# A hybrid layer in float32 on one core: its order computed anew, moving operands shifted to start on 16 bytes, inverses grown four heads at a time, and sums over tiles issued in one go

## The chip, the core and the metric

The kernel runs on one core of a Trainium2 chip. The core has five engines, each with its own queue of instructions that it works through strictly in order: PE (TensorE, the products), DVE (VectorE), ACT (ScalarE), POOL (GpSimd) and SP (which issues the transfers). An instruction that waits for a semaphore holds up everything behind it on its engine. The metric is the device time of one execution in microseconds (us); lower is better.

## What is computed

One layer of a hybrid encoder on 512 tokens behind 16 learned meta tokens, width 1024, all in float32. Cut to what matters here:

```python
u = rmsnorm(h); proj = u @ w_in                      # 1024 x 10256
y_conf = silu(layernorm(causal_dwconv31(c_val * sigmoid(c_gate)))) @ w_conf_out
q, k, v = silu(causal_dwconv4(q, k, v)); q, k = l2norm(q), l2norm(k)
o = chunk_gated_delta_rule(q, k, v, g, beta)         # 8 heads; each chunk needs (I + a_kk)^-1
y_dn = (rmsnorm(o) * silu(z)) @ w_dn_out
h = h + (sigmoid(g_conf) * y_conf + sigmoid(g_dn) * y_dn) @ w_out
u2 = rmsnorm(h); up = causal_dwconv3(u2 @ w_up)      # 1024 x 5632
h = h + (silu(f_gate) * f_val) @ w_down              # 2816 x 1024
return rmsnorm(h)[:, 16:]
```

## The kernel before

**Large products.** Features lie on the 128 partitions and tokens along the free dimension. Every weight block is loaded as a raw tile `wr`, cast by ACT to `wh` and reduced by DVE to the rest `wl`; activations are split in the same way (`uh`/`ul`, `oh`/`ol`, `hh`/`hl`, and so on). A product is the sum of three: (wh, high), (wh, low), (wl, high). The helper `gemm` (L483) issues them: for each of 8 k-tiles and 3 pairs, one PE product for each of two token ranges, so 48 products to an output tile of 128 features, in two PSUM banks (pool `p2`, two such tiles). The two ranges are what the change shifts. `FULL`, `RAW` and `HALO` (264 or 268 columns; tiles k, q, v, cg, cv) already start on multiples of 4 elements, which is 16 bytes. `LATE` and `MIDR` (L539, 258 columns; tiles z and ga, y and wo) start the first range on such a multiple and the second 8 bytes behind one. `UPR` (L1144, 258 columns; the 44 tiles `up` of the feed-forward layer) starts both 8 bytes behind one. The `dn` tiles take 512 aligned columns, the last of them 2 x 256.

**Inverses.** For each of the 8 heads there are four chunks of 128 tokens, and for each chunk a triangular matrix of 128 x 128 has to be inverted. DVE does the 32 x 32 blocks of all heads together (`inverses`, L812); they come back through memory as the tile `DU`. `grow` (L856), called once for each head, makes 64 and then 128 out of 32: DVE transposes blocks into `LL`, ACT copies blocks into `Mn[h]` (tile `mn`), PE makes the 32 x 32 products `gP`, ACT moves them out as `gp`, PE makes the 32 x 32 products `gX`, ACT moves these into `LL` and `mn`, then the same with 64 x 64 (`gP`, moved as `p`, then `gX`). All of them use a part of the PE array (32 x 32 or 64 x 64); the large products use all of it (128 x 128). A head is 8 + 12 products of 32 x 32 and 4 + 4 of 64 x 64.

**Sums.** Sums over the 128 partitions are PE products with 32 columns of ones (tile `rs`, array 128 x 32). The norm of the first four heads takes 32 of them, that of the last four 16, the two sums of the conformer's layer norm 32 each (`sums`, L501).

**What sets the order.** The program is first recorded, call by call. `Plan.order` (L273) then runs a list scheduler: an engine that comes free takes the ready call of the lowest number, where numbers are the place in the recording plus a table of offsets (`BIAS`), and ready is worked out from prices (`Plan.price`) and latencies. `STAY` is added to a large product's number while PE is in a run of small ones. The result is fixed at build time: each engine's queue. `plan.after` makes a call depend on more than its operands. PSUM tiles of one bank (`p1`) have four slots, `wh` and `wl` two each.

The profile names one line, L427, for all instructions, so that they are told apart by tile and shape. The line that issues them and the loop that calls `grow` are these:

```python
                getattr(engines[o.eng], o.fn)(*(get(x) for x in o.a), **{n: get(x) for n, x in o.k.items()})
...
    for h in range(GROW):
        call(grow, "w", h)
    for h in range(H):
        heads(h)
        if h + GROW < H:
            call(grow, "w", h + GROW)
```

Of the kernel before, what the change touches and what calls it, by code (L numbers as in the profile page):

```python
# [11 lines left out]
F32 = mybir.dt.float32  # L12
# [54 lines left out]
class Vw:  # L67
    """a view of a tile: the steps to it, and the same steps taken on a stand-in to know its bounds"""
# [52 lines left out]
class Op:  # L121
    _fields = ("eng", "fn", "a", "k", "prio", "deps", "succ", "late", "wait", "cost", "ready", "end", "tiles", "lat", "table")
# [11 lines left out]
TABLES = {'Exp': ('exp',), 'Tanh': ('exp', 'silu'), 'Silu': ('silu',), 'Sqrt': ('sqrt',)}  # L134
LAT = {'PE': {'PE': 3, 'DVE': 200, 'ACT': 200, 'POOL': 200, 'SP': 200},
# [15 lines left out]
BIAS = {'k3': -850, 'iv': -1500, 'd0': 150, 'v4': -30, 'v2': 0, 'd7': 1500, 'z1': -320, 't11': -280, 'z5': 0, 't7': 250, 'k0': -250, 'ln': 250, 's7': 30, 'z0': -700, 'o2': -250, 'o5': 100, 'd5': -1850, 'g3': 150, 'd6': -250, 'd1': 2130, 'k2': -30, 'q7': -1720, 'k5': -30, 's4': -730, 'd4': 850, 'w3': -1600, 't2': -600, 'c5': -130, 't8': 60, 'v3': 250, 'o4': -600, 'q6': -250, 'g4': -350, 't4': -100, 'o1': 250, 'q4': -630, 't9': -150, 'z2': -600, 'o0': -600, 'g0': 30, 'q3': 250, 'q5': 700, 'c1': 30, 'c6': -130, 's1': 0, 't15': 200, 't1': -700, 's3': 100, 'y0': 250, 't12': -150, 'o6': 100, 'o3': 250, 'k4': -100, 'w2': 250, 't5': -250, 'v0': 30}  # L151
LNP = 74
IVP = 1265
UP = 519
WP = 144
# [39 lines left out]
class Plan:  # L195
# [18 lines left out]
    def add(self, eng, fn, a, k):  # L214
# [30 lines left out]
        if eng == "ACT" and fn == "activation":  # L245
            o.table = TABLES.get(str(k["func"]).split(".")[-1])
# [1044 lines left out]
```

## Time and profile before

| | us |
|---|---|
| timed runs (3), median | 1048.68 |
| timed runs, lowest and highest | 1046.71, 1049.07 |
| profiled execution, first to last instruction (span) | 1049.7 |
| PE busy in it | 1035.5 |
| DVE busy | 718.3 |
| ACT busy | 474.7 |

The profiled execution has no time of its own beside its span; the span is 1.0 us above the timed median, so a difference worked out on the span is taken over to the median as it is. Busy time is the union of instructions that overlap: a product's record is some 0.28 us long while the next one starts 0.12 us behind it, so what a product costs is read from the distance of starts, not from its duration. A float32 product leaves two records, one in the split form (fp32r) leaves one. The granted clock (PEclk) is 1.00 at 2.4 GHz and 0.50 at 1.2 GHz.

The stages: first norm and keys (0 to 70 us), conformer input and inverses of 32 x 32 (70 to 222), heads with the growth of their inverses (222 to 485), layer norm and outputs (485 to 660), feed-forward layer up (660 to 915) and down (915 to 1037), a tail with the last norm.

### The profile page before, as it was taken

The page shows a single profiled execution, that of the slowest core. Times are in us where ns is not written, and L with a number is a line of the kernel's source. Part 1 is how long each engine was busy: PE and PEld are TensorE (multiplying, and loading weights), DVE is VectorE, ACT ScalarE, POOL GpSimd, SP SyncE. Part 2 cuts the span into 40 slices and gives each one's busy share as a digit, 9 for nine tenths or more (in the row PEclk, how much of TensorE's full clock was granted, in tenths as well). Part 3 has the DMA queues.
Part 4 walks back from the last instruction along what each step waited for, and adds up shares of the span by engine and source line. Part 5 has one row for each costly group of instructions (what it writes and reads, how often), then busy time and mean ns, then how long its engine had stood idle before and what let it go on. Part 6 is the DMA issues. An engine that isn't in the chain of part 4 may idle for free.

```text
span 1049.7 us, 20033 instructions
## 1 busy us (share of the span) xinstructions
PE 1035.5 (99%) x8430; PEld 985.7 (94%) x8430; DVE 718.3 (68%) x1237; ACT 474.7 (45%) x863; POOL 9.5 (1%) x45
## 2 busy tenths in 40 slices
PE   9999999999999999999999999999999999999996
PEld 7999999988989999999999999999999999988885
DVE  6987899984867998985546555666666767623324
ACT  6777622557534466444345234534444443413222
POOL 0011000000000000000000000000000000000000
PEclk9999999987999999999999999999999999999998
DMA  6244323231211232212313343232323232333232
GB/s 223 76 123 110 114 82 111 81 102 42 71 42 61 81 106 98 78 65 76 127 61 122 101 143 99 81 102 81 100 81 101 81 101 81 96 91 91 81 105 81
DMA packets 44042, 98.40 MB, mean 94 GB/s; under 512 B 12720, under 2 KB 19248, under 8 KB 43952
## 3 DMA queue, kind: packets, MB, share of 16 engines
q1 hardware_dynamic: 43952, 97.12, 29.2%
q8 instruction: 66, 1.08, 0.4%
q14 instruction: 24, 0.20, 0.1%
HBM read 93.89 MB, written 3.21 MB: 93 GB/s over the span
## 4 chain that ended last, share of the span: by engine, by line
PE 96%; DVE 1%; ACT 1%; DMA 0%; SPq 0%; issue 0%; POOL 0%; DVEq 0%; POOLq 0%; ACTq 0%
PE up L427 24%; PE dn L427 12%; PE ga L427 9%; PE y L427 9%; PE k L427 5%; PE v L427 5%; PE z L427 5%; PE q L427 4%; PE wo L427 4%; PE cv L427 4%; PE cg L427 4%; PE rs L427 2%; PE o L427 2%; PE gX L427 1%; PE S L427 1%; PE gP L427 1%
## 5 line engine op out<-in xcount | busy, mean ns | idle before, releaser
L427 DVE TENSOR_TENSOR wl<-wr,wh 128x1024 fp32r<-128x1024 f32 x157 | 189.3, 1207 | 160.1 <-PE dn L427 47.8
L427 ACT CAST wh<-wr 128x1024 fp32r<-128x1024 f32 x157 | 162.0, 1037 | 287.5 <-PE up L427 87.8
L427 DVE SCALAR_TENSOR_TENSOR ca<-c,par,ca 128x516 f32<-128x516 f32 (+10 forms) x240 | 177.3, 744 | 7.3 <-ACT ca L427 4.8
L427 PE MATMUL up<-hl,wh 128*128 128x258 f32 x704 | 142.1, 283 | 0.0
L427 PE MATMUL up<-hh,wh 128*128 128x258 f32 x704 | 142.1, 283 | 0.0
L427 PEld LDWEIGHTS up<-hh,wh 128*128 128x128 f32 x704 | 109.0, 190 | 0.2 <-issue 0.2
L427 PEld LDWEIGHTS up<-hl,wh 128*128 128x128 f32 x704 | 108.9, 189 | 0.0
L427 PE MATMUL up<-hh,wl 128*128 128x258 f32 x704 | 92.4, 283 | 0.0
L427 PEld LDWEIGHTS up<-hh,wl 128*128 128x128 f32 x704 | 88.3, 189 | 0.0
L427 DVE TENSOR_TENSOR up<-up,r 128x258 f32<-128x258 f32 x88 | 33.4, 420 | 49.0 <-PE up L427 46.0
L427 DVE SCALAR_TENSOR_TENSOR uy<-up,par,uy 128x512 f32<-128x512 f32 x88 | 65.9, 748 | 1.5
L427 PE MATMUL dn<-fh,wh 128*128 128x512 f32 (+1 forms) x198 | 65.0, 369 | 0.0
L427 PE MATMUL dn<-fl,wh 128*128 128x512 f32 (+1 forms) x198 | 64.9, 369 | 0.0
L427 ACT ACTIVATE uy<-up,par 128x512 f32<-128x512 f32 x44 | 36.0, 817 | 53.8 <-DVE up L427 53.8
L427 PE MATMUL ga<-uh,wh 128*128 128x258 f32 x256 | 58.5, 290 | 0.0
L427 PE MATMUL ga<-ul,wh 128*128 128x258 f32 x256 | 57.9, 289 | 0.0
L427 DVE SCALAR_TENSOR_TENSOR cv<-ra,par,cv 128x528 f32<-128x528 f32 x69 | 51.6, 760 | 0.6 <-ACT cv L427 0.5
L427 PE MATMUL dn<-fh,wl 128*128 128x512 f32 (+1 forms) x198 | 49.8, 370 | 0.0
L427 PE MATMUL ga<-uh,wl 128*128 128x258 f32 x256 | 48.4, 299 | 0.0
L427 PEld LDWEIGHTS dn<-fh,wh 128*128 128x128 f32 x198 | 36.9, 188 | 7.8 <-ACT wh L427 1.2
L427 PEld LDWEIGHTS dn<-fl,wh 128*128 128x128 f32 x198 | 36.9, 188 | 6.9
L427 PEld LDWEIGHTS ga<-ul,wh 128*128 128x128 f32 x256 | 42.2, 189 | 0.8 <-issue 0.6
(284 smaller groups left out, 2238.9 us busy)
## 6 DMA issues: line engine op xcount, KB each, us to landing
wr<-in_win SPq DMA_DIRECT2D x64, 512.0 KB, 3.3
wr<-in_wup SPq DMA_DIRECT2D x44, 512.0 KB, 3.7
wr<-in_wd SPq DMA_DIRECT2D x17, 512.0 KB, 3.6
wr<-in_wdn SPq DMA_DIRECT2D x8, 512.0 KB, 3.2
wr<-in_wco SPq DMA_DIRECT2D x8, 512.0 KB, 3.4
wr<-in_wo SPq DMA_DIRECT2D x8, 512.0 KB, 3.3
wr<-in_wd SPq DMA_DIRECT2D x8, 384.0 KB, 3.1
x<-in_xT SPq DMA_DIRECT2D x8, 264.0 KB, 5.8
```

Of the source, the lines that this page charges most:

```text
L427: getattr(engines[o.eng], o.fn)(*(get(x) for x in o.a), **{n: get(x) for n, x in o.k.items()})
```

## The change

Four things, all in the recording; no product is added or removed, and the counts of PE products by array part are the same (6930 split ones, 790 in float32).

1. `UPR` moves by two elements (the tiles `hh`/`hl` are written two columns later), so that both ranges start on 16 bytes. In `LATE` and `MIDR` the second range starts two columns earlier and is 260 long, the first is written two columns into its bank, and what reads the banks takes columns 2 to 260 of both.
2. `grow` does four heads in a call (two calls instead of eight). Each group of products waits until everything that the group reads has been written (`written`). ACT moves a whole group out at once.
3. The sums of the heads' norms and of the layer norm wait until all their tiles are there.
4. The scheduler's prices, `STAY` (3000 to 750), the offsets of stages and the clock's thresholds are new, and with them the order on every engine. Of the table of offsets nothing is shown; its rows tell a reader nothing.

```diff
-LOW = 0.4
+RATE = 0.4453
+TURN = {(False, True): 92, (True, False): 105, (True, True): 190}
+LOW = 0.5
...
-STAY = 3000
+STAY = 750
...
-IVP = 1265
+IVP = 1295
...
-WP = 144
+WP = 30
...
-GROW = 3
+NG = 4
...
-            for b, (c0, c1) in enumerate(ranges):
-                PE.matmul(acc[:, b, :c1 - c0], lhsT=w[:, k * P:(k + 1) * P], rhs=a[k0 + k][:, c0:c1],
+            for b, (c0, c1, *at) in enumerate(ranges):
+                p0 = at[0] if at else 0
+                PE.matmul(acc[:, b, p0:p0 + c1 - c0], lhsT=w[:, k * P:(k + 1) * P], rhs=a[k0 + k][:, c0:c1],
                           start=first and i == 0, stop=last and i == len(runs) - 1)
...
-    def sums(ss, width):
+    def sums(ss, width, whole=False):
+        if whole:
+            plan.after = {j for t in ss for _, j, w in t.tl.hist if w}
...
-    LATE = ((PAD + T0, PAD + T0 + HW), (PAD + T0 + HW, PAD + T))
-    MIDR = ((0, HW), (HW, TW))
+    LATE = ((PAD + T0, PAD + T0 + HW, 2), (PAD + T0 + HW - 2, PAD + T, 0))
+    MIDR = ((0, HW, 2), (HW - 2, TW, 0))
+    MID = slice(2, 2 + HW)
...
-    def grow(h):
...
+    def grow(h0):
+        hs, DU = range(h0, h0 + NG), ivt['DU']
+        LL = []
+        for h in hs[::2]:
             l = bt(n="LL")[:, :8 * 64].rearrange("p (q c) -> p q c", q=8)
             G.memset(l[0:32, :, 32:64], 0.0)
             for r, c in ((0, 0), (32, 32), (64, 0)):
                 V.transpose(out=l[r:r + 32, :, c:c + 32], in_=DU[r:r + 32, NC * h:NC * h + 8])
+            LL.append(l)
+        D8 = lambda h: DU[:, NC * h:NC * h + NC]
+        for h in hs:
+            for b in range(4):
+                r = slice(32 * b, 32 * b + 32)
+                S.copy(out=Mn[h][r, :, r], in_=D8(h)[r])
+        def written(*ts):
+            plan.after = {j for t in ts for _, j, w in t.tl.hist if w}
+        each = [(h, q, (h - h0) * NC + q) for h in hs for q in range(NC)]
         a = p1("gP")
+        written(*LL, *(Mn[h] for h in hs))
+        for h, q, i in each:
+            c, l = slice(i * 32, (i + 1) * 32), LL[i // 8][:, i % 8]
+            PE.matmul(a[32:64, c], lhsT=Mn[h][0:32, q, 32:64], rhs=l[0:32, 0:32], start=True, stop=True)
+            PE.matmul(a[96:128, c], lhsT=Mn[h][64:96, q, 96:128], rhs=l[64:96, 0:32], start=True, stop=True, tile_position=(64, 96))
+        pp = bt(n="gp")
+        n = NG * NC * 32
+        for r in (slice(32, 64), slice(96, 128)):
+            S.copy(out=pp[r, :n], in_=a[r, :n])
         x = p1("gX")
+        written(pp)
+        for h, q, i in each:
+            c, d = slice(i * 32, (i + 1) * 32), D8(h)
+            PE.matmul(x[0:32, c], lhsT=pp[32:64, c], rhs=d[32:64, q], start=True, stop=True)
+            PE.matmul(x[64:96, c], lhsT=pp[96:128, c], rhs=d[96:128, q], start=True, stop=True, tile_position=(96, 64))
+            PE.matmul(x[32:64, c], lhsT=d[32:64, q], rhs=pp[32:64, c], start=True, stop=True)
+        x8 = x[:, :n].rearrange("p (q i) -> p q i", i=32)
+        for i, l in enumerate(LL):
+            S.copy(out=l[32:64, :, 0:32], in_=x8[32:64, 8 * i:8 * i + 8])
+        for h in hs:
+            for r, c in ((slice(0, 32), slice(32, 64)), (slice(64, 96), slice(96, 128))):
+                S.copy(out=Mn[h][r, :, c], in_=x8[r, (h - h0) * NC:(h - h0 + 1) * NC])
+        p64s = []
+        for g in range(NG // 2):
+            a = p1("gP2")
+            written(*LL, *(Mn[h] for h in hs))
+            for h, q, i in each[8 * g:8 * g + 8]:
+                PE.matmul(a[64:128, i % 8 * 64:i % 8 * 64 + 64], lhsT=Mn[h][0:64, q, 64:128], rhs=LL[g][0:64, i % 8], start=True, stop=True)
+            p64 = bt(n="p64")
+            S.copy(out=p64[64:128, :512], in_=a[64:128])
+            p64s.append(p64)
+        for g in range(NG // 2):
+            x = p1("gX2")
+            written(*p64s)
+            for h, q, i in each[8 * g:8 * g + 8]:
+                c = slice(i % 8 * 64, i % 8 * 64 + 64)
+                PE.matmul(x[0:64, c], lhsT=p64s[g][64:128, c], rhs=Mn[h][64:128, q, 64:128], start=True, stop=True)
+            for h in hs[2 * g:2 * g + 2]:
+                S.copy(out=Mn[h][0:64, :, 64:128], in_=x[0:64, (h % 2) * 256:(h % 2 + 1) * 256].rearrange("p (q i) -> p q i", q=NC))
...
+                plan.after = {j for pair in st_r for t in pair for _, j, w in t.tl.hist if w}
...
-    for h in range(GROW):
-        call(grow, "w", h)
+    call(grow, "w", 0)
     for h in range(H):
         heads(h)
-        if h + GROW < H:
-            call(grow, "w", h + GROW)
+        if h == 0:
+            call(grow, "w", NG)
...
-        acc, r = sums(cacc[::-1], TW)
+        acc, r = sums(cacc[::-1], TW, True)
...
-        rl = rstd_sb(sq, TW, 1.0 / D, eps, "rl")
+        rl = rstd_sb(sq, TW, 1.0 / D, eps, "rl", True)
...
+    HS = 2
...
-        S.mul(out=hi[:, :TW], in_=x[:, :TW], mul=pc('nf', f))
-        V.scalar_tensor_tensor(out=lo[:, :TW], in0=x[:, :TW], scalar=pc('nf', f), in1=hi.bitcast(F32)[:, :TW],
+        S.mul(out=hi[:, HS:HS + TW], in_=x[:, :TW], mul=pc('nf', f))
+        V.scalar_tensor_tensor(out=lo[:, HS:HS + TW], in0=x[:, :TW], scalar=pc('nf', f), in1=hi.bitcast(F32)[:, HS:HS + TW],
                                op0=ALU.mult, op1=ALU.subtract)
         hh.append(hi)
...
-    UPR = ((2, 260), (258, 516))
+    UPR = ((HS + 2, HS + 260), (HS + 258, HS + 516))
```

What this does to the queues is seen in three places. `DU`, `gp`, `mn`, `LL` are the tiles named above; `hsel` are the columns of ones for the heads' sums, `o` and `q` the squares that are summed.

**PE, the sums of the first four heads.** Before:

```order
L427 MATMUL S_3_3811<-w_6_3801,kdm_930 128x128
L427 MATMUL o_3_3813<-Em_1000,w_6_3801 128x16
L427 MATMUL gX_3817<-DU_2902,gp_3805 32x32
L427 MATMUL rs_3819<-o_1_3454,hsel_71 32x129
L427 MATMUL gX_3817<-DU_2902,gp_3805 32x32
L427 MATMUL rs_3819<-o_1_3454,hsel_71 32x129
L427 MATMUL gX_3817<-gp_3805,DU_2902 32x32
```

Now:

```order
L447 MATMUL v_4520<-uh_101,wh_4339 128x264
L447 MATMUL rs_4548<-o_1_3506,hsel_71 32x129 x4
L447 MATMUL rs_4548<-q_1_2428,hsel_71 32x129 x4
L447 MATMUL rs_4548<-o_2_3740,hsel_71 32x129 x4
L447 MATMUL rs_4548<-q_2_3440,hsel_71 32x129 x4
L447 MATMUL rs_4548<-o_3_4228,hsel_71 32x129 x4
L447 MATMUL rs_4548<-q_3_3585,hsel_71 32x129 x4
L447 MATMUL rs_4548<-o_4_4535,hsel_71 32x129 x4
L447 MATMUL rs_4548<-q_4_4389,hsel_71 32x129 x4
L447 MATMUL w_9_4586<-v_5_4551,Tm_2216 16x128
```

Before, 24 of these 32 sums stand one by one between products of the growth (16 in this place, 8 in a second one); now all 32 stand together, and the 16 of the last four heads too.

**PE, the growth of the first heads, from the 32 x 32 products to the 64 x 64 ones.** Before:

```order
L427 MATMUL gX_3059<-DU_2902,gp_3043 32x32 x2
L427 MATMUL gX_3059<-gp_3043,DU_2902 32x32
L427 MATMUL ga_2915<-ul_121,wh_2850 128x258
L427 MATMUL ga_2915<-uh_125,wh_2850 128x258 x2
L427 MATMUL ga_2915<-ul_127,wh_2850 128x258 x2
L427 MATMUL ga_2915<-uh_87,wl_2874 128x258
L427 MATMUL gP_1_3096<-LL_2943,mn_1096 64x64 x4
L427 MATMUL gP_2_3102<-LL_2950,mn_1351 64x64 x4
L427 MATMUL ga_2915<-uh_87,wl_2874 128x258
```

Now:

```order
L447 MATMUL gX_3126<-DU_2909,gp_3116 32x32 x2
L447 MATMUL gX_3126<-gp_3116,DU_2909 32x32
L447 MATMUL gP_1_3203<-LL_2994,mn_1059 64x64 x4
L447 MATMUL gP_1_3203<-LL_2994,mn_1138 64x64 x4
L447 MATMUL gP_2_3216<-LL_3000,mn_1200 64x64 x4
L447 MATMUL gP_2_3216<-LL_3000,mn_1234 64x64 x4
L447 MATMUL z_3229<-uh_87,wh_2981 128x258
L447 MATMUL z_3229<-uh_87,wh_2981 128x260
L447 MATMUL z_3229<-ul_90,wh_2981 128x258
L447 MATMUL z_3229<-ul_90,wh_2981 128x260
L447 MATMUL z_3229<-uh_93,wh_2981 128x258
L447 MATMUL gX_1_3241<-mn_1059,p_1_3227 64x64 x4
```

Before, products of `ga` stand between the last `gX` of 32 x 32 and the first `gP` of 64 x 64; now nothing stands there.

**ACT, beside the same place.** Before:

```order
L427 COPY mn_1430<-DU_2902 32x4x32
L427 COPY LL_2943<-gX_3028 32x4x32
L427 COPY mn_1096<-gX_3028 32x4x32 x2
L427 COPY LL_2943<-gX_3049 32x4x32
L427 COPY mn_1247<-gX_3049 32x4x32
L427 COPY LL_2950<-gX_3059 32x4x32
L427 COPY mn_1351<-gX_3059 32x4x32 x2
L427 COPY mn_1247<-gX_3049 32x4x32
L427 COPY mn_1430<-DU_2902 32x4x32 x2
L427 COPY p_1_3112<-gP_2_3102 64x256
```

Now:

```order
L447 COPY gp_3116<-gP_3073 32x512 x2
L447 COPY mn_1616<-DU_2909 32x4x32 x3
L447 COPY mn_1702<-DU_2909 32x4x32 x4
L447 COPY mn_1750<-DU_2909 32x4x32 x4
L447 COPY LL_2994<-gX_3126 32x8x32
L447 COPY LL_3000<-gX_3126 32x8x32
L447 COPY mn_1059<-gX_3126 32x4x32 x2
L447 COPY mn_1138<-gX_3126 32x4x32 x2
L447 COPY mn_1200<-gX_3126 32x4x32 x2
L447 COPY mn_1234<-gX_3126 32x4x32 x2
L447 CAST wh_3201<-wr_2903 128x1024
L447 ACTIVATE gt_3225<-ga_2919,par_69 128x516
```

Before, the copies out of `gX` follow each other with one block copy from `DU` among them; now eleven block copies for the second four heads stand between `gp` and the ten copies that the 64 x 64 products read.

At the end of the queues the norm of the first half of the tokens is moved forward as well: its four products `rb` stand 38 products before the last `dn` one (before: behind it), and so the eight DVE products `fin` of that half stand ahead of the last addition to `xr` instead of behind it.

## Rows read from the trace of the kernel before

**Rows 1.** The page: PE's busy time, its granted clock in slices, the chain.

```profile
PE 1035.5 (99%) x8430; PEld 985.7 (94%) x8430; DVE 718.3 (68%) x1237; ACT 474.7 (45%) x863; POOL 9.5 (1%) x45
...
PEclk9999999987999999999999999999999999999998
...
PE 96%; DVE 1%; ACT 1%; DMA 0%; SPq 0%; issue 0%; POOL 0%; DVEq 0%; POOLq 0%; ACTq 0%
```

**Rows 2.** Windows (stretch, length, busy and count by engine, PEclk, DMA, GB/s), growth.

```profile
230.60:244.20 13.60, 13.60 (x112) 12.13 (x111) 4.88 (x8) 9.10 (x25) 0.00 (x0) 0.50 0.07 23
...
254.50:261.30 6.80, 6.80 (x37) 6.20 (x37) 3.71 (x7) 3.92 (x11) 0.34 (x2) 0.50 0.19 42
```

**Rows 3.** Windows, stretches of products of 264, 258 (wo), 258 (up), 512 columns.

```profile
126.00:176.00 50.00, 50.00 (x413) 50.00 (x412) 48.01 (x130) 11.94 (x15) 0.00 (x0) 1.00 0.33 112
626.00:660.00 34.00, 34.00 (x286) 34.00 (x285) 19.07 (x24) 13.22 (x18) 0.00 (x0) 1.00 0.29 93
700.00:900.00 200.00, 200.00 (x1657) 200.00 (x1656) 136.11 (x207) 82.11 (x103) 0.00 (x0) 1.00 0.28 92
940.00:1000.00 60.00, 60.00 (x260) 48.18 (x259) 17.75 (x20) 16.75 (x20) 0.00 (x0) 1.00 0.33 96
```

**Rows 4.** Timeline of PE (start, length, instruction, count): sums among the growth's products.

```profile
291.14 0.24 PE L427 MATMUL gX<-DU,gp 32*32 32x32 f32 x2
...
291.65 0.24 PE L427 MATMUL gX<-DU,gp 32*32 32x32 f32 x2
...
299.56 0.39 PE L427 MATMUL z<-uh,wh 128*128 128x258 f32 x1
...
319.62 0.41 PE L427 MATMUL rs<-o,hsel 128*32 128x129 f32 x2
```

**Rows 5.** Timeline of PE: the 36 sums that stand together.

```profile
484.68 0.45 PE L427 MATMUL rs<-o,hsel 128*32 128x129 f32 x8
...
486.82 0.39 PE L427 MATMUL ga<-ul,wh 128*128 128x258 f32 x1
```

**Rows 6.** Timeline of PE: into a small product's part of the array and back.

```profile
223.75 0.28 PE L427 MATMUL q<-uh,wl 128*128 128x264 f32 x1
223.97 0.31 PE L427 MATMUL gP<-LL,mn 32*32 32x32 f32 x4
224.21 0.39 PE L427 MATMUL ga<-ul,wh 128*128 128x258 f32 x1
```

**Rows 7.** Timeline of PE: runs of small products, and a wait among them.

```profile
227.66 0.21 PE L427 MATMUL gX<-DU,gp 32*32 32x32 f32 x1 [0.46 <-ACT gp L427]
...
231.79 1.11 PE L427 MATMUL gP<-LL,mn 64*64 64x64 f32 x8
...
251.53 0.70 PE L427 MATMUL gP<-LL,mn 32*32 32x32 f32 x32
```

**Rows 8.** Timeline of ACT: the growth's copies, and a bank moved out.

```profile
222.05 3.52 ACT L427 COPY mn<-DU 32x128 f32<-32x128 f32 x15 [0.54 <-DMA DU<-d_x]
...
228.20 0.52 ACT L427 COPY mn<-gX 32x128 f32<-32x128 f32 x2
...
305.22 0.60 ACT L427 ACTIVATE z<-z 128x516 f32<-128x516 f32 x1 [1.58 <-PE z L427]
```

**Rows 9.** Timeline of PE, DVE and ACT: the tail.

```profile
1036.67 1.08 PE L427 MATMUL rb<-rr,cst 128*128 128x64 f32 x8
...
1037.78 2.74 DVE L427 TENSOR_TENSOR fin<-xr,rb 128x256 f32<-128x256 f32 x8 [0.60 <-PE rb L427]
1038.08 0.31 ACT L427 ACTIVATE rr<-rs,eps 128x64 f32<-128x64 f32 x1
...
1040.44 0.55 DVE L427 RECIPROCAL rr<-rr 128x64 f32<-128x64 f32 x1
1041.13 1.94 PE L427 MATMUL rb<-rr,cst 128*128 128x64 f32 x8 [3.13 <-DVE rr L427]
```

More of the change, by code (lines that the diff above doesn't have):

```diff
@@ L121 @@
 class Op:
-    _fields = ("eng", "fn", "a", "k", "prio", "deps", "succ", "late", "wait", "cost", "ready", "end", "tiles", "lat", "table")
+    _fields = ("eng", "fn", "a", "k", "prio", "deps", "succ", "late", "wait", "cost", "ready", "end", "tiles", "lat", "table", "mode", "act", "tail", "alone")
 class Rec:
@@ L241, in add @@
         o.deps, o.succ, o.table = deps, [], None
-        o.part = eng == "PE" and fn == "matmul" and (writes[0].shape[0] < P or args[1].shape[0] < P) and writes[0].shape[0] % 32 == 0
-        o.share = args[1].shape[0] / P if o.part else 1.0
+        o.mode = None
+        if eng == "PE" and fn == "matmul":
+            up = lambda n: 32 if n <= 32 else 64 if n <= 64 else P
+            o.mode = (up(args[1].shape[0]), up(writes[0].shape[0]))
+            o.mode = None if o.mode == (P, P) else o.mode
         o.cost, o.lat = self.price(eng, fn, a, k, writes[0])
+        o.alone = self.price(eng, fn, a, k, writes[0], True)[0] if o.mode else o.cost
+        o.act = (args[2].n if writes[0] is args[0] else args[1].n) / 0.6 * o.mode[0] / P if o.mode else o.cost
+        o.tail = 950 + (2800 if fn == "dma_start" and o.lat > 700 and self.run(k) <= P else 0)
         if eng == "ACT" and fn == "activation":
@@ L247, in add, with run, price @@
         self.ops.append(o)
-    def price(self, eng, fn, a, k, out):
+    @staticmethod
+    def run(k):
+        return min(v.ap.ap[-1][1] if v.ap.ap[-1][0] == 1 else 1 for v in (k["out"], k["in_"]))
+    def price(self, eng, fn, a, k, out, alone=False):
         n = out.n
@@ L255, in price @@
                 return 110, 0
-            if out.ap.offset // out.tl.row:
+            if out.ap.offset // out.tl.row and not alone:
                 return 22, 0
-            return max(n, lhs.n) / 2.4 * (1 if lhs.tl.dt == F32R else 4) + 3, 0
+            if lhs.tl.dt == F32R:
+                return RATE * n + 4 + (2 if rhs.ap.offset % rhs.tl.row % 4 else 0), 0
+            if lhs.shape[0] == 64:
+                return 115, 0
+            return max(n, lhs.n) / 0.6 + 8, 0
         if fn == "dma_start":
-            runs = [v.ap.ap[-1][1] if v.ap.ap[-1][0] == 1 else 1 for v in (k["out"], k["in_"])]
-            return 475, int(np.prod(out.shape)) * 4 / 360.0 * (1 if min(runs) > 127 else 2)
+            return 475, int(np.prod(out.shape)) * 4 / 290.0 * (1 if self.run(k) >= P else 2)
         aps = sum(isinstance(k.get(x), Vw) for x in ("scalar", "scalar1", "scalar2", "scale", "bias", "mul"))
@@ L333, in look @@
                     continue
-                if e == "PE" and not o.part:
-                    st = max(st, drain)
                 if st > t:
@@ L338, in look @@
                     continue
-                if e == "PE" and part and not o.part:
+                if e == "PE" and mode and o.mode != mode:
                     p += STAY
@@ L388, in order @@
             if e == "SP":
-                dma = max(dma, t + 1100) + o.lat
-                o.end = dma + 950
+                dma = max(dma, t + 950) + o.lat
+                o.end = dma + o.tail
             out.append(i)
@@ L520, in spread, with rstd_rows @@
         return t
[L522 removed]
+    def rstd_rows(ss, width, scale, bias, whole=False):
         q = width // 4
[L525 removed]
+        acc, r = sums(ss, width, whole)
         S.activation(out=r[:, :q], in_=acc[:, :q], func=AF.Sqrt, bias=bias, scale=scale)
@@ L528, in rstd_rows, with rstd_sb @@
         return r
-    def rstd_sb(ss, width, scale, bias, n):
-        return spread(rstd_rows(ss, width, scale, bias), width, n)
+    def rstd_sb(ss, width, scale, bias, n, whole=False):
+        return spread(rstd_rows(ss, width, scale, bias, whole), width, n)
     def halves(ap, w):
@@ L884, in grow @@
-        x8 = x[:, :NC * 32].rearrange("p (q i) -> p q i", q=NC)
-        S.copy(out=L8[32:64, :, 0:32], in_=x8[32:64])
-        S.copy(out=M8[0:32, :, 32:64], in_=x8[0:32])
-        S.copy(out=M8[64:96, :, 96:128], in_=x8[64:96])
-        a = p1("gP2")
-        for q in range(NC):
-            PE.matmul(a[64:128, q * 64:(q + 1) * 64], lhsT=M8[0:64, q, 64:128], rhs=L8[0:64, q], start=True, stop=True)
-        p64 = bt(n="p64")[:, :NC * 64]
-        S.copy(out=p64[64:128], in_=a[64:128, :NC * 64])
@@ L893, in grow @@
-        x = p1("gX2")
-        for q in range(NC):
-            PE.matmul(x[0:64, q * 64:(q + 1) * 64], lhsT=p64[64:128, q * 64:(q + 1) * 64], rhs=M8[64:128, q, 64:128], start=True, stop=True)
-        S.copy(out=M8[0:64, :, 64:128], in_=x[0:64, :NC * 64].rearrange("p (q i) -> p q i", q=NC))
+            LL.append(l)
[4 more added lines that the diff above has]
+                S.copy(out=Mn[h][r, :, r], in_=D8(h)[r])
```

48 lines of the change are left out of this document (15 added, 33 removed).

## The prediction

> **What bounds the kernel now.** I read the page first. PE is busy for 1035.5 of 1049.7 us, and the chain that ended last runs through PE for 96% of the span [rows 1]. Busy time hides stalls shorter than a product's own length, so the next view is the windows: how many products start in a stretch of like ones, at which granted clock. In most of the span they start at an even distance and the clock is full; the dips are two stretches at 1.2 GHz in the growth of the inverses [rows 2] and the tail. So PE's queue is the bound, and the time is the sum of what stands in it: products at their distance, the turns between parts of the array, stretches at half clock, and the few waits. DVE comes next: 48.0 of 50 us in the conformer's input stage [rows 3].
>
> **The change part by part.** Negative is a gain.
>
> *Starts on 16 bytes.* A window's count holds every product that touches it, so the distance is (length + one product's 0.28) / count. Of 264 columns, all aligned: 50.28 / 413 = 121.7 ns. Of 512: 60.28 / 260 = 231.9, so a column costs 110.2 / 248 = 0.444 ns, and 258 aligned columns should take 121.7 - 2.7 = 119.0. The `up` products, all unaligned, take 200.28 / 1657 = 120.9; the `wo` products, every second one unaligned, 34.28 / 286 = 119.9, just between [rows 3]. So an unaligned start costs 1.9 ns. Gain on 2112 `up` products: 1.9 x 2112 = 4.0 us. The other 48 tiles (ga, y, z, wo) have 1152 pairs; each saves 1.9 and pays two columns, 0.9: 1.1 us. The first of each pair now writes its bank from byte 8; no row shows a split product doing so. Its price lies between nothing and that of an operand's unaligned start, 1.9 x 1152 = 2.2 us; I take nothing, since banks are written, not read, and keep the end. **-5.1**, ends 0 and -6.
>
> The rows of equal width and unequal start differ [rows 3]. The Trainium skill (TensorE: Matmul & The Clock Gate, Back-to-back issue gap) gives the distance from the number of columns alone. It speaks against this part: by it the starts bring nothing. It is a rival below.
>
> *Sums in one go.* Between 291.14 and 299.56 a sum and a product of the growth alternate; one such pair takes 291.65 - 291.14 = 0.51 us, as each turns the array twice, and there are 16. Eight more begin at 319.62 [rows 4]. Together 24 x 0.51 = 12.2 us. In a run, 36 sums take 486.82 - 484.68 = 2.14 us [rows 5], 59 ns each: 24 cost 1.4. The 24 partners in a run cost 0.70 / 16 = 0.044 us each [rows 7]: 1.1. **-9.7**. The sums now wait for all of their tiles; what queues behind the first of them on PE is the current large product. The last tile comes from ACT's square of head 3 (or DVE's addition of head 7), and both sums stand later in PE's queue than their first pieces did, so I price that wait at nothing; if the cover is gone, a wait of one ACT instruction, 0.6 us [rows 8], twice.
>
> *Fewer turns.* Counted in the queue, the part of the array changes 226 times before and 148 times after. Of the 78, 48 are the alternations above; of the other 30, 28 are in the growth and 10 at sums, and the start has 8 more. A turn into a small product costs 223.97 - 223.75 - 0.12 = 0.10 us, the way back 0.24 for two products of 0.04 and the turn, 0.16 [rows 6]; about 0.12. 30 x 0.12: **-3.6**.
>
> *The growth in one call.* Here the change adds waits. PE's queue after the first four heads' 32 x 32 `gP` holds 8 products of q, 8 x 0.12 = 1.0 us; ACT moves `gp` out in two copies of 512 columns, as long as the one of 516, 0.60 each [rows 8], and with about 0.2 for handing over PE waits some 0.4. Then PE runs 48 `gX` products, three runs of 0.70 less two tails of 0.2, 1.7 us [rows 7], and behind them stands `gP` of 64 x 64, with nothing between. It waits for ACT, whose queue holds: 11 block copies at 3.52 / 15 = 0.235, 2.6 us; two to `LL` of 256 columns, between 0.26 and 0.60, some 0.37, 0.7; eight to `mn` at 0.26, 2.1 [rows 8]. That is 5.4, against 1.7 of PE: a wait of 3.7 us, and all of PE's queue stands behind it (z is not the cover: it is queued later, and its bank is freed by ACT's `gt`, also behind those copies). The second `gX` follows after 5 products of z, which are about as long as the two copies of `p`. The second call has large products between its groups. One wait of 0.46 before goes [rows 7]. **+3.6**, ends 0 and +6.
>
> *The clock.* Before, PE stood at half clock for 13.6 + 6.8 = 20.4 us [rows 2], which cost half of it, 10.2. After, the first call packs small products and a wait of nearly 4 us; before, less than that (small products with `ga` among them) took the clock down at 230.6. So I expect it to fall during the wait. What follows at half clock: 16 products `gP` of 64 x 64 at 1.11 for four [rows 7], 4.4 with tails; five of z, 1.2; 16 `gX`, 4.4; 32 `gP` of the next heads, twice 1.2; then mixed work. Before, the clock rose some 6 us after the dense small products had ended. 12 + 5 = 17 us, 8.5 lost. The second call is spread among large products and I expect no second fall. **-1.7**, ends -10 (it never falls) and +2 (a second fall of 6.8 us).
>
> *The tail.* The second half's reciprocal is ready to start when ACT's root ends, 1038.39, but DVE is at the first half's eight `fin` until 1040.5 [rows 9]. These now stand ahead: -1.9. The last `rb` may then find the full clock, 1.08 instead of 1.94 [rows 9]: 0 to -0.9. The first half's `rb`, now among products instead of in the gap behind the last one, costs its 1.08. **-1.3**.
>
> *The rest of the order.* The new queue is tighter. A PSUM tile of two banks is refilled within 11 records of PE work after its predecessor's end at ten places instead of four, the nearest after 6 instead of 8. Six are 0.7 us, and moving out takes 0.60 [rows 8] plus handing over both ways, so I take 0.2 for each of six, 1.2 us, with 0 and 3 as ends. In the heads' chain about half of the gaps from `wP` to the next product with `w` lost one product; 0.3. At the start the first weight's load now follows the first input tile; DVE's list up to the growth is the same but for one `wl`. I price these at nothing; the cover is that both are loaded before PE needs either. **+1.5**.
>
> Sum: -5.1 - 9.7 - 3.6 + 3.6 - 1.7 - 1.3 + 1.5 = -16.3. The profiled span of 1049.7 becomes 1033.4; the median of the timed runs lies 1.0 below the span, so **1032.4 us**. Less than 0.2%, some 2 us, can't be told from no change.
>
> **The rivals.**
>
> *The starts bring nothing.* Then 1152 products are only two columns longer, 1152 x 0.9 ns = 1.0 us, and the 5.1 are missing: 1032.4 + 6.1 = 1038.5. For it: what tells 119.0 from 120.9 is an interpolation over 6 columns. Against it: `wo` lies just between. The Trainium skill's rule on the issue gap, above, would have it so.
>
> *PE's new queue stands tighter than DVE and ACT can serve.* Where DVE is busy for 48.0 of 50 us [rows 3], a rest `wl` (1.2 us) that comes late stops PE. Four to eight such places, or the ten bank refills at 0.6 each, cost 6 us: 1038 to 1040. Against it: before, PE waited almost nowhere with the same lists.
>
> *The burst is harmless.* The clock stays up, or other work fills the wait: -8.5 and up to -1: 1023.
>
> *The clock stays low through both calls: slower.* The second call's 48 `gX` come only 43 products after the first call's end. If the clock has not risen by then, the stretch runs on to the end of the second call: 162 products, some 17 us at full clock (80 small ones 5.5, 60 split ones 7.3, 20 in float32 4.4), 34 at half. 12 + 34 + 5 = 51 us at 1.2 GHz lose 25.5 instead of 8.5, and with a wait of 6 at its upper end it is 1032.4 + 17 + 2.4 = 1051.8. The point from which it decides is whether those 43 products, 10 us at half clock, raise the clock. Against it: before, it rose twice after no more than that.
>
> **How the numbers follow.** Forecast 0.45, its own range 1027 to 1037 from the ends of the growth, the clock and the refills; the starts bring nothing 0.20; tighter queue 0.17; harmless burst 0.10; clock low through both 0.08. The range leaves out the last and the edges of two others: 1022 to 1042. Faster by over 0.2% are all but the last and a sliver of the tight queue: 0.89; within 0.2%: 0.04; slower: 0.07.
>
> **What would show it.** In the windows over `up`, 119.0 ns instead of 120.9. No alternation of `rs` with `gX`, the 32 sums in about 1.9 us. A wait of PE for ACT of nearly 4 us before the first 64 x 64 products, and one stretch of about 17 us at 1.2 GHz behind it. The last `rb` some 1.5 us after the root. Wrong would be: an unchanged distance, a second fall of the clock, or PE waits elsewhere that sum to over 3 us.

## The result and the profile after

The changed kernel takes 1037.4 us (median of 4, 1036.81 to 1037.96), the kernel before 1047.7 beside it (1046.06 to 1049.07): a ratio of 0.9891, with a 95% interval of 0.9869 to 0.9913. It is 10.3 us faster where I had forecast 16.3, and the time lies inside the range (1022 to 1042), 5.0 us above the forecast of 1032.4.

The page of the profile after: PE's share, the granted clock in slices, the chain that ended last. They answer to [rows 1].

```profile
PE 1019.7 (98%) x8430; PEld 978.8 (95%) x8430; DVE 717.1 (69%) x1237; ACT 476.7 (46%) x847; POOL 8.4 (1%) x45
...
PEclk9999999997999999999999999999999999999998
...
PE 92%; DVE 3%; ACT 3%; DMA 1%; issue 1%; SPq 0%; POOL 0%; DVEq 0%; ACTq 0%; POOLq 0%
```

PE's queue is still the bound. Of the two dips of the clock in the growth one is left. The windows over that dip and over 200 us of `up` products (columns as in [rows 2]):

```profile
241.64:255.29 13.65, 12.99 (x147) 12.39 (x144) 6.78 (x11) 7.95 (x20) 0.10 (x1) 0.50 0.18 59
...
690.00:890.00 200.00, 200.00 (x1669) 200.00 (x1669) 136.51 (x208) 83.40 (x105) 0.00 (x0) 1.00 0.27 93
```

By the count, `up` now starts every 200.28 / 1669 = 120.0 ns, against 120.9 in [rows 3]. The timeline of PE after, from the start over the growth of the first four heads and the sums to the tail:

```profile
24.22 1.06 PE L447 MATMUL rc<-rr,cst 128*128 128x132 f32 x8
...
50.68 0.48 PE L447 MATMUL k<-xh,wh 128*128 128x264 f32 x2 [0.59 <-DVE g L447]
...
235.06 1.20 PE L447 MATMUL gP<-LL,mn 32*32 32x32 f32 x64
236.19 1.24 PE L447 MATMUL q<-uh,wl 128*128 128x264 f32 x8
237.36 0.39 PE L447 MATMUL gX<-DU,gp 32*32 32x32 f32 x3
...
241.41 3.45 PE L447 MATMUL gP<-LL,mn 64*64 64x64 f32 x32 [2.67 <-ACT LL L447]
245.51 0.80 PE L447 MATMUL z<-uh,wh 128*128 128x258 f32 x2 [0.66 <-ACT gt L447]
...
353.31 0.43 PE L447 MATMUL rs<-o,hsel 128*32 128x129 f32 x8
...
355.21 0.39 PE L447 MATMUL w<-v,Tm 16*16 16x128 f32 x2
...
1018.89 1.00 PE L447 MATMUL rb<-rr,cst 128*128 128x64 f32 x8
...
1026.84 1.94 PE L447 MATMUL rb<-rr,cst 128*128 128x64 f32 x8 [1.11 <-DVE rr L447]
```

and ACT's, beside the wait of 2.67 us:

```profile
237.51 3.36 ACT L447 COPY mn<-DU 32x128 f32<-32x128 f32 x11
240.90 0.63 ACT L447 COPY LL<-gX 32x256 f32<-32x256 f32 x2
241.55 2.12 ACT L447 COPY mn<-gX 32x128 f32<-32x128 f32 x8
```

The 32 sums stand in a row and take 355.21 - 353.31 = 1.9 us. The wait that I had named is there, before the first 64 x 64 products, and ACT's eleven block copies stand in front of `LL`. What is seen only now: `rc`, which spreads the first norm, starts at 24.22 where the trace before has it at 23.06, and two products of the keys wait a little behind it (the 0.59 at 50.68, and 0.18 at 57.53).

The two traces split at the `up` products. Before, these begin (first product with `hl`) at 656.1 and end at 910.4; after, at 645.1 and 897.8. So 11.0 us were won ahead of them, 254.3 - 252.7 = 1.6 in them and 1.7 behind: 14.3 on the span. The timed runs show 10.3. That difference is the subject of the first experiment.

### The profile page after: what moved, and what is told of

Its sections match the earlier page's. It is cut to its first block, busy times and chain, and to the rows that moved or that the text cites. A ratio compares the mean times of both kernels' runs of the same rounds, so it can differ in the third digit from the quotient of the medians.

```text
span 1035.4 us, 20014 instructions
## 1 busy us (share of the span) xinstructions
PE 1019.7 (98%) x8430; PEld 978.8 (95%) x8430; DVE 717.1 (69%) x1237; ACT 476.7 (46%) x847; POOL 8.4 (1%) x45
## 4 chain that ended last, share of the span: by engine, by line
PE 92%; DVE 3%; ACT 3%; DMA 1%; issue 1%; SPq 0%; POOL 0%; DVEq 0%; ACTq 0%; POOLq 0%
PE up L447 25%; PE dn L447 12%; PE ga L447 9%; PE y L447 9%; PE z L447 5%; PE v L447 5%; PE wo L447 5%; PE q L447 4%; PE cv L447 4%; PE cg L447 3%; PE k L447 2%; PE o L447 2%; PE rs L447 1%; PE S L447 1%; PE wP L447 1%; DVE cv L447 1%
## 5 line engine op out<-in xcount | busy, mean ns | idle before, releaser
L447 DVE SCALAR_TENSOR_TENSOR ca<-c,par,ca 128x516 f32<-128x516 f32 (+13 forms) x240 | 175.5, 742 | 3.1 <-ACT ca L447 0.3
L447 PE MATMUL dn<-fh,wh 128*128 128x512 f32 (+1 forms) x198 | 71.7, 370 | 0.0
L447 PE MATMUL dn<-fl,wh 128*128 128x512 f32 (+1 forms) x198 | 71.2, 368 | 0.0
L447 PE MATMUL ga<-uh,wh 128*128 128x258 f32 (+1 forms) x256 | 56.9, 287 | 0.0
L447 PE MATMUL ga<-ul,wh 128*128 128x258 f32 (+1 forms) x256 | 56.6, 288 | 0.0
L447 PE MATMUL dn<-fh,wl 128*128 128x512 f32 (+1 forms) x198 | 45.4, 369 | 0.0
L447 PE MATMUL ga<-uh,wl 128*128 128x258 f32 (+1 forms) x256 | 44.6, 289 | 0.0
L447 PEld LDWEIGHTS ga<-uh,wh 128*128 128x128 f32 x256 | 42.1, 190 | 0.2
```

## The experiments

**A second trace of the kernel before.**

> The kernel before, unchanged, for a second trace of it. The timed runs of it lie between 1046.06 and 1049.07 us, those of the changed kernel between 1036.81 and 1037.96, so something in the kernel before differs from one execution to the next. Theory 1: the second stretch at half clock (6.8 us at 254.5) does not come in every execution; with and without it the times differ by 3.4 us, and a trace of an execution near 1046 has one stretch only. Theory 2: the clock is the same each time and the 3 us lie in waits for transfers in the first 70 us. By the changed kernel, whose device time is 1.7 us above its span, I expect a span between 1044 and 1047.

Its span is 1047.0 us, with 1048.69 us for the median of 10 timed runs beside it. The windows at half clock:

```profile
234.80:241.63 6.83, 6.59 (x36) 6.22 (x33) 1.78 (x4) 5.86 (x15) 0.00 (x0) 0.50 0.12 36
251.87:258.69 6.82, 6.82 (x37) 6.05 (x36) 3.88 (x7) 3.85 (x11) 0.34 (x2) 0.50 0.13 42
```

13.65 us at 1.2 GHz in place of the 20.4 of [rows 2], with the same program: 3.4 us of lost time less, and the span is 2.7 us shorter. Theory 1 holds in kind: the clock varies from one execution to the next (not that a stretch is missing, the first is half as long). The Trainium skill (TensorE: Matmul & The Clock Gate, Part 1: The HAM clock gate) says as well that the point where the clock changes differs between runs of one kernel; the two traces agree (the first fall comes at 230.6 us in one and at 234.8 in the other). The timed runs fit: over 42 of them beside the experiments, the kernel before takes 1043.57 us at a mean granted clock of 0.996 and 1053.55 us at 0.982, and the longer runs have the lower clock (correlation -0.96). So the trace that I predicted from had more half clock than the next one. In the runs where both are known the device time is 1.75 us above the span (1037.14 and 1035.4 in the changed kernel), not 1.0 below it.

The changed kernel traced again:

> The changed kernel again, for a second trace, beside e8_head. Timed runs between 1036.8 and 1038.0 as before, span 1.75 us below. If what varies between executions of the kernel before is the clock in the growth, and the changed kernel's stretch at half clock is always 13.65 us, its times spread over less than 2 us; the wait of kt for DVE at 74 us (0.85 us in its first trace, 2.6 to 2.9 in e1_starts, e2_nowait and e3_act, 0.6 in e7_fill) would be the second thing that varies, by 2 us.

1036.33 us (six runs, 1035.53 to 1040.58), span 1034.6, again 13.65 us at half clock and `kt` waiting 0.8 us. The two waits of the growth in it:

```profile
240.58 2.81 PE L447 MATMUL gP<-LL,mn 64*64 64x64 f32 x32 [2.67 <-ACT LL L447]
244.70 0.80 PE L447 MATMUL z<-uh,wh 128*128 128x258 f32 x2 [1.30 <-ACT gt L447]
```

Five of the six lie within 0.9 us and one is 4 us longer; what varies in that one isn't known. That `kt` varies is shown by the seven traces (this one, the first and five of the experiments below) whose queues are the same up to there: it waits 0.43 to 0.76 us in four of them and 2.37 to 2.79 in three (e1_starts, e2_nowait, e3_act). PE waits for DVE, and DVE for a transfer, first in the changed kernel's first trace, then in e1_starts:

```profile
72.67 1.63 DVE L447 SCALAR_TENSOR_TENSOR Em<-Em,gc,cst 16x16 f32<-16x16 f32 x8 [2.04 <-DMA Em<-d_gm]
...
74.11 2.00 DVE L449 SCALAR_TENSOR_TENSOR Em<-Em,gc,cst 16x16 f32<-16x16 f32 x8 [3.78 <-DMA Em<-d_gm]
...
76.76 0.80 PE L449 MATMUL kt<-cst,cv 128*128 128x128 f32 x4 [2.79 <-DVE Mm L449]
```

Neither trace of the kernel before has a wait there. So the new order has put a transfer on PE's path, and it costs up to 2.8 us in some executions.

**The sums gathered, and nothing else.** In the kernel before, PE's queue alone is changed (here and below the lists of calls have names that say what they hold, and the lines that collect them are left out):

```diff
     seq = plan.order()
+    for g in heads_sums:        # 32 and 16 products rs
+        last = max(map(seq.index, g))
+        seq = [i for i in seq[:last + 1] if i not in g] + g + seq[last + 1:]
```

> The kernel before with one move on PE alone: the products of the heads' sums (32 and 16) are gathered in the place of the last of them; every other instruction of every engine stands where it stood. By the prediction 24 alternations of 0.51 us (12.2) become 24 sums of 59 ns and 24 growth products at 44 ns (2.5): -9.7 us. Rival: the products of the growth and the chain behind them (ACT's copies, then the 64 x 64 products) were waited for in that stretch anyway, so that the time comes back as a wait behind it: -3 to -5 us.

1036.94 us (1033.65 to 1040.23), ratio 0.9893 [0.9873, 0.9913]: 11.0 us faster than before, as much as the whole change. In its trace the sums, on PE's timeline:

```profile
358.50 0.43 PE L438 MATMUL rs<-o,hsel 128*32 128x129 f32 x8
...
360.40 0.39 PE L438 MATMUL z<-ul,wh 128*128 128x258 f32 x1
```

and the one window at half clock in the growth:

```profile
233.91:240.74 6.83, 6.75 (x54) 6.27 (x55) 1.70 (x3) 6.03 (x16) 0.00 (x0) 0.50 0.14 40
```

`up` begins at 639.6 us, 13.9 ahead of the second trace of before. Right ahead of the alternations the two are already 3.4 apart: 0.7 from the start, the rest from the second stretch at half clock, which this execution doesn't have. The other 10.5 are the alternations. The forecast of 9.7 was right, and the rival falls: no wait behind the growth takes the time back.

**The wait for all tiles.** The changed kernel without the line that makes the heads' sums wait:

```diff
-                plan.after = {j for pair in st_r for t in pair for _, j, w in t.tl.hist if w}
```

> The changed kernel without the wait of the heads' sums for all of their tiles (the order is computed anew, and moves a little on PE, DVE, ACT and SP behind the growth). In the new queue the sums then stand in eight groups of 4 or 8 instead of two of 32 and 16, each a turn of the array and back, and none alternates with products of the growth. Theory 1 (the new prices keep them apart from the growth, the wait only bundles them): six more turns both ways at some 0.26 us, +1.6 us. Theory 2 (the wait is what removes the alternation): 9.7 us come back.

1040.63 us (1038.97 to 1043.57), 3 to 4 us above the changed kernel, and no sum alternates with products of the growth: the first eight stand together between two groups of it (at 274.36), the others behind it. The turns at sums cost 1.6 us more in its trace (worked out over all products: distance of starts less the even distance). The other part isn't the sums: this execution was at half clock for 17.1 us in the growth and for 3.4 at 76 us, behind a wait of 2.37 at `kt`. So the wait in the code is worth the 1.6; what removes the alternation is the new queue, in which the growth's last product starts at 277.1 us (before: 350.1), before the last tiles come. Which part of the change moves the growth forward, its four heads in a call or the scheduler's numbers, no run shows.

**The starts.** The changed kernel with all ranges as before and the same order on each engine:

```diff
-    LATE = ((PAD + T0, PAD + T0 + HW, 2), (PAD + T0 + HW - 2, PAD + T, 0))
+    LATE = ((PAD + T0, PAD + T0 + HW), (PAD + T0 + HW, PAD + T))
...
-    HS = 2
+    HS = 0
```

> The changed kernel with the starts of the ranges as before (up: 258 columns, both 8 bytes behind a multiple of 16; z, ga, y, wo: 258 and 258, the second one unaligned, banks written from their first column), and the same order on every engine. By the prediction (an unaligned start costs 1.9 ns, two more columns 0.9, the later start in the bank nothing): up at 120.9 instead of 119.0, time +5.1 us. What the trace of the changed kernel shows, 120.0 for up instead of 120.8 before, and 119.4 and 121.6 for the pairs instead of 119.1 and 121.4, says: up +1.75 us, the pairs -0.6 to -0.9, together +0.9 to +1.2 us, hardly measurable. Rival (the starts are nothing, and up's 0.8 ns came from something else in the new order): up stays at 120.0 in this kernel.

1038.91 us (1037.45 to 1041.51). The times can't give the price of the starts: the traced execution also has the wait of 2.79 at `kt` and 3.4 us at half clock behind it. The distances can. Windows over `up`, first of this kernel:

```profile
690.00:890.00 200.00, 200.00 (x1656) 200.00 (x1655) 136.97 (x209) 81.94 (x103) 0.00 (x0) 1.00 0.26 90
```

200.28 / 1656 = 120.9 ns against 120.0: the starts are worth 0.9 x 2112 = 2.0 us here. The pairs give nothing: a pair of `ga`, from the first start to the next pair's, is 240.6 ns here and 240.7 in the changed kernel. The same window of e2_nowait, whose `up` has the same starts and lengths as the changed kernel's:

```profile
690.00:890.00 200.00, 200.00 (x1664) 200.00 (x1663) 136.45 (x208) 82.92 (x104) 0.00 (x0) 1.00 0.27 93
```

That is 120.4. And of the next kernel, with aligned starts in the order of before:

```profile
690.00:890.00 200.00, 200.00 (x1653) 200.00 (x1653) 136.04 (x207) 82.72 (x104) 0.00 (x0) 1.00 0.26 90
```

121.2, more than the 120.9 of the unaligned starts before (and than the 120.8 of e4_gather, which has the same order on PE and unaligned starts). So the start alone doesn't set the price. Within one kernel every `up` tile takes the same time (within 0.1 ns a product, but for one or two), and the eight `hh` and `hl` differ among themselves by 4 ns and more a product; what changes between these kernels is where those tiles lie in SBUF. That it is the place is only argued: no trace shows a tile's place, and no run moves the tiles alone.

The eleven forms:

> The changed kernel with the 44 up tiles in eleven forms, four tiles each (192 products a form), same order: columns and start of the moving operand, start in the bank. Theory 1 (four columns, 16 bytes, go at once; a product takes as long as the groups it touches, and an unaligned start costs 0.8 ns): 258 and 260 aligned both 120.0, 262 and 264 aligned both 121.8, 258 unaligned 120.8, 260 and 262 unaligned 122.6. Theory 2 (0.444 ns for each column, 0.8 for an unaligned start): 258, 260, 262, 264 aligned 120.0, 120.9, 121.8, 122.7; 258, 260, 262 unaligned 120.8, 121.7, 122.6. For the bank: written from byte 8, 258 and 260 aligned cost nothing more (as I predicted), or 0.3 to 1.2 ns more (as the pairs in the changed kernel's trace suggest). Some columns are computed that nothing reads, so a few results differ in what their halo holds.

Each form reads its columns from other places than the layer does, so its values aren't the layer's; the number of products is (one run, 1038.99 us). Distances of starts within a form, means of some 188 each, standard error 0.2 ns:

| columns | aligned | unaligned | aligned, bank from byte 8 |
|---|---|---|---|
| 258 | 120.0 | 120.8 | 119.9 |
| 260 | 121.3 | 121.8 | 120.7 |
| 262 | 122.5 | 121.5 | |
| 264 | 121.3 | | |

Neither theory stands: 264 columns are cheaper than 262, and at 262 the unaligned start is the cheaper one. The later start in the bank costs nothing, as I had assumed. The mixed forms show what misled me: aligned then unaligned gives 118.6 and 121.5, whose mean is 120.1. The distance between two starts isn't the first product's price.

**Three moves in the order of before.** The gathered sums, aligned `up` (tiles two columns later) and, at the end of DVE's queue:

```diff
+    seq = [i for i in seq if i not in fin_first_half]
+    at = seq.index(reciprocal_second_half) + 1
+    seq[at:at] = fin_first_half
```

> The kernel before with three moves and its own order otherwise: the heads' sums gathered (as in e4_gather), the ranges of up on 16 bytes (tiles written two columns later), and on DVE the second half's reciprocal ahead of the first half's eight fin at the very end. Growth, start and the order of the heads stay those of before. If the gains add (gathering -11.0 as measured, up 2112 x 0.83 ns = -1.8, the tail -1.5): 1033.7 us, and the rest of the change (growth four heads at a time, its start, its order) then costs 3.7 us against the changed kernel's 1037.4. Rival (the growth in one call and the new order are worth what the prediction gave them, so that the whole change must be better than these three): it can't be faster than 1037.4.

1036.41 us (1035.85 to 1040.35). The gains don't add to 1033.7: `up` gained nothing (121.2, above), and this execution was at half clock for 13.65 us in the growth where e4_gather's had 6.83. From the last addition to `xr` to the end of the span it takes 1035.18 - 1023.79 = 11.4 us, before 1049.67 - 1036.76 = 12.9: the tail's move is right in itself. Against the rival: three moves are as good as the whole change, so the new growth and the new order together were worth nothing measurable. By the spans they rather cost 1.3 to 2.1 us (an estimate: with the sums' 10.5, the 2.0 of `up` that this kernel lacks and the tail's 1.2, the second trace's 1047.0 would become 1033.3, and the changed kernel's two traces have 1034.6 and 1035.4; all these have 13.65 us at half clock in the growth).

**ACT's queue in the growth.** In the changed kernel, eleven copies moved:

```diff
-    gp x2, mn<-DU x11, LL x2, mn<-gX x8, wh, gt, p x2
+    gp x2, LL x2, mn<-gX x8, wh, gt, p x2, mn<-DU x11
```

> The changed kernel with eleven instructions moved on ACT alone: the block copies mn<-DU of the second four heads, which stand between gp and LL in the growth of the first four, stand behind the two copies of p instead. PE, DVE, POOL and SP keep their order. Theory 1 (these copies make PE's wait of 2.67 us before the 64 x 64 products): the wait shrinks to 0.9, what is left of handing over and of LL's first copy, and the time falls by 1.8 us if the clock falls as before. Theory 2 (it is the wait that takes the clock down): with 0.9 the stretch at half clock (some 13.5 us, 6.7 lost) goes too, -8.5 in all. Theory 3 (the second four heads' 32 x 32 products now wait for the moved copies, 3.4 us of ACT): what is gained comes back there, between 0 and +2 us.

1035.76 us (1035.21 to 1036.99). In its trace the first `gP` and PE's two waits on the timeline:

```profile
236.79 1.20 PE L461 MATMUL gP<-LL,mn 32*32 32x32 f32 x64
...
241.09 2.52 PE L461 MATMUL gP<-LL,mn 64*64 64x64 f32 x32 [0.61 <-ACT LL L461]
245.20 0.80 PE L461 MATMUL z<-uh,wh 128*128 128x258 f32 x2 [1.60 <-ACT gt L461]
```

and the window at half clock:

```profile
242.45:256.10 13.65, 12.05 (x132) 11.46 (x131) 6.95 (x11) 10.39 (x28) 0.10 (x1) 0.50 0.20 59
```

The eleven copies are the wait: 2.67 becomes 0.61. The wait at `z` grows from 0.66 to 1.60, since `gt` still stands behind `mn` and the cast of `wh`, but nothing comes back by that: the clock fell later, so the 64 x 64 products ahead of it took 2.52 us in place of 3.45. From the first `gP` to `z` it takes 245.20 - 236.79 = 8.41 us here, against 10.45 and 10.47 in the two traces of the changed kernel: all of the 2.0 us are won. That the time falls by only 0.6 to 1.6 fits the wait at `kt`, 2.45 us in this trace. And the clock falls as before, so a wait of 2.67 isn't needed to take it down.

**The growth filled.** All sixteen copies and the cast behind `p`, and large products of `q` behind `gP` and `gX`:

```diff
 ACT
-    mn<-DU x5 ... gp x2, mn<-DU x11, LL x2, mn<-gX x8, wh, gt, p x2
+    gp x2, LL x2, mn<-gX x8, gt, p x2, wh, mn<-DU x16
 PE
-    q x11, gP x32, q x8, gX x48, gP 64 x 64
+    gP x32, q x13, gX x48, q x6, gP 64 x 64
```

> The changed kernel with the growth of the first four heads filled: on ACT all sixteen block copies of the second four heads and the cast of a weight stand behind the copies of p; on PE eleven products of q that stood ahead of the 32 x 32 gP stand behind it, and six products of q stand behind gX. Nothing else moves. Theory 1 (the waits are ACT's queue, and the clock falls by the small products whatever PE waits): the waits of 2.67 and 0.66 us shrink to some 0.5 in sum, the stretch at half clock stays 13.65 us, 1034.6 us. Theory 2 (the wait takes the clock down): the stretch is 6.8 us or gone, -3.4 to -6.8 more, 1028 to 1031 us. Theory 3 (the sixteen copies, 4.9 us of ACT, are now waited for by the second four heads' gP): what is gained comes back, 1037 us.

1034.18 us (1033.86 to 1034.55), ratio 0.9860 [0.9821, 0.9899]: faster than both kernels by more than their spread, 2.2 to 3.2 us below the changed one. PE's timeline:

```profile
234.20 1.20 PE L478 MATMUL gP<-LL,mn 32*32 32x32 f32 x64
...
238.25 1.00 PE L478 MATMUL q<-uh,wl 128*128 128x264 f32 x6
239.18 2.08 PE L478 MATMUL gP<-LL,mn 64*64 64x64 f32 x32
241.99 0.60 PE L478 MATMUL z<-uh,wh 128*128 128x258 f32 x2 [0.74 <-ACT gt L478]
...
249.62 0.80 PE L478 MATMUL wP<-r,mn 128*128 128x128 f32 x2 [0.94 <-ACT mn L478]
```

and the window at half clock:

```profile
242.26:252.50 10.24, 9.30 (x115) 8.82 (x114) 6.70 (x11) 9.57 (x27) 0.10 (x1) 0.50 0.24 79
```

Theory 1: no wait stands before the 64 x 64 products any more, and the clock still falls behind them (10.24 us, in this execution). From the first `gP` to `z` it takes 7.79 us, with eleven more products of `q` in it (1.3 us), against 10.45 and 10.47: 4.0 us won. A wait of 0.94 has come up at `wP`, for copies that now stand behind the sixteen, and gives part of it back. The stretch at half clock is 3.4 us shorter, but that isn't a further gain: in the changed kernel its first 3 to 4 us lie over products and a wait that end with ACT's `gt` in any case, and from `z` on it is 9.8 and 10.5 us there. Theory 3 is out: the second four heads' `gP` doesn't wait.

**The start.** The same kernel with the first 340 calls in the order of before:

```diff
     seq = plan.order()
+    seq = HEAD + [i for i in seq if i not in HEAD]    # HEAD: the first 340 calls of before's order
```

> e7_fill with the first 340 calls (the loads, the first norm and the first two key tiles, some 30 us) in the order of the kernel before, everything else in the order of e7_fill. In the trace of before PE reaches the products rc, which spread the norm, at 23.5 us, in the changed kernel at 25.0, with eight turns of the array more. Theory 1 (the new order of the start costs 1.5 us there, and up to 3 with the two waits behind it at 50 and 57 us): rc at 23.5, 1031.2 to 1032.7 us. Theory 2 (a later wait for the first keys takes it back, as the rest of the order was computed for the other start): rc at 23.5, but 1034.2 us.

1036.49 us (1034.55 to 1037.53). PE's timeline of the start:

```profile
23.27 1.06 PE L495 MATMUL rc<-rr,cst 128*128 128x132 f32 x8
...
50.17 0.51 PE L495 MATMUL k<-xh,wh 128*128 128x264 f32 x2 [1.94 <-ACT wh L495]
...
56.69 0.39 PE L495 MATMUL gp<-g__1_750,cst 128*128 128x40 f32 x2 [0.83 <-DVE g__1_750 L495]
```

`rc` comes 1.6 us earlier than in e7_fill (24.90), and then PE waits 1.94 us for a cast and 0.83 for DVE, and the clock is at half for 3.4 us behind the first of these: theory 2, and worse, since the time is 2.3 us above e7_fill's. This part of the order couldn't be put back alone. Of the 1.6 us not all is the order: `rc` starts anywhere from 23.32 to 24.90 in seven traces with the new start (the changed kernel's second has 23.32), and from 22.09 to 23.06 in four with the old one. By the means, 24.1 and 22.7, the new start costs the changed kernel 1.4 us at `rc`, and 0.8 behind it; that it could be had for nothing isn't shown.

## Why the prediction was right in sign and too large

By its steps, against the first traces where they are alike:

- **The base.** The step that failed first is "the median lies 1.0 below the span, so". The span of the changed kernel was forecast as 1033.4 and is 1035.4; the median was forecast as 1032.4 and is 1037.4. So 3.0 of the 5.0 us are the base: the one traced execution of before had 3.4 us more of half clock than the next one, and I took its offset to the median for a constant.
- **Starts on 16 bytes: forecast -5.1, measured -2.0.** The step "258 aligned columns should take 119.0" failed. The line through 264 and 512 columns doesn't hold within a few columns (the form gives 120.0), and the `wo` rows, "just between", were the mean of a pair, which says nothing on either (35 of the 286 in that window are `up` products besides). The 1.1 us of the pairs are 0. The end 0 of the range was the likelier end, and e5_three shows even that end. The rival that the starts bring nothing (1038.5) came closest to the time, partly by the base, so by luck. The Trainium skill's rule (TensorE: Matmul & The Clock Gate, Back-to-back issue gap), by which the number of columns alone decides, would give 258 / 2.4 + 2.5 = 110.0 ns, an estimate; the traces disagree, with 120.0 to 121.2 for the same 258 columns, and starts are only one of what it leaves out.
- **Sums in one go: forecast -9.7, measured -10.5** by e4_gather, 1.9 us for the 32. Right, and nothing waits for them. It is the whole change's gain.
- **Fewer turns: forecast -3.6.** Not measured alone. In e2_nowait six turns both ways cost 1.6 us, 0.13 a turn, near the 0.12 taken (the mean of the 0.10 and 0.16 that I had read is 0.13 as well). What the other terms leave of the 14.3 us between the first two traces (2.0 + 10.5 - 2.9 + 3.4 + 1.2 - 1.4 = 12.8) is 1.5; that is a remainder, with every other term's error in it.
- **The growth in one call: forecast +3.6, measured +2.9** (2.67 + 0.66 - 0.46; in the second trace 2.67 + 1.30 - 0.46 = 3.5). Place, order and engine were right. The sizes: eleven copies took 3.36 us, not 2.6; the eight `mn` copies weren't waited for, since the first 64 x 64 products began at 241.41 with `mn<-gX` begun at 241.55: the code's wait for everything written sets the order alone, and on the chip a product waits for its own operands. The 0.4 of waiting for `gp` didn't come, 8 products of `q` cover it.
- **The clock: forecast one stretch of 17 us, measured one of 13.65**, in both traces, and no second fall: the rival that is slower is out, and so is the harmless burst. Against the first trace of before it is -3.4, against the second 0. It falls 0.2 us behind the end of the wait, but the reason that I gave, "during the wait", falls with e7_fill: it comes without that wait too.
- **The tail: forecast -1.3, measured -1.2**: 12.9 - (1035.36 - 1024.48) = 2.0 less from the last `xr` on, 1019.70 - 1018.89 = 0.8 for the earlier `rb`. The last `rb` took 1.94 again.
- **The rest of the order: forecast +1.5, measured +1.4, but made of other things: a hit by luck.** I had looked for banks refilled too early; of PE's waits in the trace after one of 0.23 at `cg` may be such. What I had priced at nothing, the start, costs 1.2 at `rc` and 0.59 + 0.18 behind it; `kt` waits 0.68 at 75 us and `S` 0.53 at 263. Against these 3.4 with `cg`'s stand two waits of the trace before that I had overlooked when I wrote that PE waited almost nowhere, on PE's timeline:

```profile
101.16 0.49 PE L427 MATMUL gg<-cv 128*128 128x128 f32 x2 [0.79 <-ACT kd L427]
...
108.22 0.49 PE L427 MATMUL gg<-cv 128*128 128x128 f32 x2 [1.23 <-ACT kd L427]
```

They are gone: 2.0 us that no part of the change was credited with. With `kt` at 2.4 to 2.8 us, as in three other traces, this term would have been 3.1 to 3.5: the rival of the tight queue came in part, as `k`, `kt` and `cg` wait for DVE.

## What to carry to other kernels

Look first for places where instructions of two array shapes alternate one by one: 24 such pairs held 10.5 us, and gathering them alone gives what a recomputed order with three more edits gave. When a group of small products waits for copies, read the copying engine's queue for what stands there for somebody else; moving sixteen copies and a few large products was worth another 2 to 3 us. And trace the base twice before taking a difference from its span.

## What the runs showed of the hardware

- One program stands at 1.2 GHz in the growth for 20.4 us in one execution and for 13.65 in another; the timed runs of the kernel before spread from 1043.6 to 1053.6 us.
- The clock falls behind dense small products whether PE waits 2.67 us among them or not at all ahead of the 64 x 64 ones. For 3.4 us it also fell behind a wait of PE among large products, of 1.94 us in e8_head, 2.37 in e2_nowait and 2.79 in e1_starts; behind one of 2.45 in e3_act it didn't.
- The same transfer lets DVE go on at 72.67 us in one execution and at 74.11 in another, with the same queue ahead of it (issued at 66.9 and 66.6).
- Equal products of 258 columns start every 120.0, 120.4, 120.9 or 121.2 ns in different kernels, constant within each; the start's alignment alone doesn't tell which. What does stays open.
- Products of 262 columns with aligned starts took longer (122.5 ns) than those of 264 (121.3).
